# A gated encoder layer: y transposed on all partitions at once, and the first strip begun on half of the tokens

## The chip, the cores and the metric

The kernel runs on one core of one Trainium2 chip. The metric is the device time of one execution in microseconds; the median of three runs before the change is 2567.74 us (2566.76 to 2569.13). TensorE (PE) multiplies matrices and accumulates in PSUM banks, VectorE (DVE) and ScalarE (ACT) work element by element, GpSimd (POOL) here issues transfers and computes a few powers, and SyncE (SP) issues the other transfers.

## The reference

With DEPTH = 1 only one layer is computed, a gated MLP with spatial mixing. x has 1024 tokens of 2048 channels, the inner width E is 4096, the chunks are 128 tokens and there are 8 groups of 512 channels.

```python
h = rmsnorm(x, a_norm)
z = h @ w_in                                  # (1024, 3 * 4096)
u, v, gate = split(z, 3)
u = gelu(u)
v = rmsnorm(gelu(v), v_gain)
vc = v.reshape(b, 8, 128, 8, 512)
sv = einsum('gpq,bnqgc->bnpgc', w_s, vc) + b_s
y = u * sv.reshape(b, 1024, 4096)
x = x + (y * silu(gate)) @ w_out
out = rmsnorm(x, final_norm)
```

## The kernel before

**Products.** Both large matrix products are done as Strassen's seven products of half blocks. A block is named by two digits: of the left operand, the first digit is the half of the tokens (512 of 1024) and the second the half of the inner dimension; of a weight, the first is the half of the inner dimension and the second one of two column blocks of 512. `A_OF` and `B_OF` (lines 20 and 21) give the blocks that each product adds or subtracts; `IN_ORDER` and `OUT_ORDER` the order of the products. Every operand is split into a high part that TensorE takes exactly and a low part that is the remainder (`split`, lines 84 to 87: ACT writes the high part, VectorE subtracts), and each product is three matmuls (`mm3`, lines 89 to 93: high by high, high by low, low by high).

**Steps.** The work is a list of steps (line 108). The input product has 12 strips of two column blocks: four strips of v, then eight strips that pair a group of u with the same group of gate. Each strip has seven products of JI = 4 steps; a step is 2 x 128 of the inner dimension, 24 matmuls of 128x512. The output product has seven products by two column pairs by JO = 8 steps. At each step i, `advance` first issues the loads for step i+3 (`prefetch`) and forms the operands of step i+2 (`feed`); then come the matmuls (`products`), and then `work`, which takes entries from two lists of postponed work, `soon` (taken first, all of it) and `later` (until the costs written beside the entries use up an allowance of 2.3 us, less in part of the output product).

**Banks.** PSUM is used as two sets of four banks. Products 1, 2 and 5 of a strip start on fresh banks; 4 and 7 go on accumulating on product 2's, 3 and 6 on product 5's, after `end_of` has read what it needs of the product before. In the order 1, 2, 5, 4, 3, 7, 6 the two sets alternate (lines 401 to 440).

**Start.** x comes transposed, as 16 tiles of 256 channels by 512 tokens, both halves of the tokens in turn (line 235 and following). Each tile is squared by ACT, its two parts added by VectorE and summed over the channels by a matmul with ones into `ss_x`. From the sums of both halves the reciprocal root mean square is made (`d_x`, a reduction, a power on POOL), spread over the partitions as `r_b` by a matmul with a diagonal matrix for each half, and applied to a block of x when it is first wanted (`h_block`, line 161). `feed_first` forms the first step's operands half by half so that TensorE can begin early. In the first strip each product forms its left operands and POOL writes them to DRAM (`a_dram`); the later strips read them back. Weight blocks are loaded for each product anew in the first strip; from the second on a block that two products of a strip use stays in its buffer.

**Buffers.** Tiles of 4 KB per partition come from four groups of buffers: 25 "big" (x, raw weights, read-back operands, output accumulators), 6 "hl" (split weights), 3 "sum" and 16 "ax".

**Mixing.** v is written to DRAM by strip. For each group, `spatial_step` reads it back, splits it, multiplies it by the mixing matrix, whose rows carry v's norm, and multiplies by u * silu(gate). The output product wants y with channels on partitions, so `finish_y` (line 337) transposes: for each of the 4 chunks of a half of the tokens it takes 4 parts of 32 tokens, and each part is 4 instructions on 32 partitions by 4 blocks of 32 channels. One instruction transposes 32x32 blocks within 32 partitions. The result of two chunks, 128 channel partitions by 4 by 256 tokens, is one transfer to `y_dram`. `load_y` reads it back for the output product; if the last group isn't complete by then, the postponed work is done first.

**Output.** The result is accumulated on top of x, loaded by POOL (`init_acc`, line 453). Rows are squared and summed as they are finished; `scale_rows` and `finish_rows` (line 491) multiply by the final norm and SP stores 128 rows by 512 columns at a time, 32 stores, 16 for each half of the tokens; those of the second half come after the last matmuls.

**Order.** Within an engine, instructions run in one fixed order, made when the program is built. It follows the order of the code, except that an instruction that is not expected to be ready can be passed by a later one.

Of the kernel before, what the change touches and what calls it, by code (L numbers as in the profile page):

```python
# [14 lines left out]
P = 128  # L15
# [15 lines left out]
def gmlp_kernel(ctx, tc, x, xT, g_in, w_in, gain, wsT, bsT, w_out, fnorm, out):  # L31
# [88 lines left out]
    def load_w(step, block):  # L120
        kind, s, p, j = step
        mat, cols, n = (w_in, strips, JI) if kind == "in" else (w_out, outs, JO)
        cached = kind == "in" and s > 0
        key = (kind, s, 0 if cached else p, block, j)
        if key not in wraw:
            k = ((block // 10 - 1) * n + j) * 2 * P
            col = cols[s][block % 10 - 1]
            wraw[key] = slot("big", "w_raw")
            nc.sync.dma_start(
                out=wraw[key], in_=mat[k:k + 2 * P, col:col + C].rearrange("(u p) c -> p u c", p=P))  # L130
        return wraw[key]

    def load_y(step, block):
        _, _, p, j = step
        key = (p, block, j)
        if key not in yraw:
            g, b = divmod(((block % 10 - 1) * JO + j) * 2, CB)
            if g == G - 1 and pairs_of_y[0] < 4 * G:
# [35 lines left out]
    def feed_first():  # L174

        step = steps[0]
        (a1, _, a2), (b1, _, b2) = A_OF[step[2]], B_OF[step[2]]
        aparts[0] = [slot("ax", f"a_{l}", F32R) for l in ("hi", "lo")]
        wparts[0] = [slot("hl", f"w_{l}", F32R) for l in ("hi", "lo")]
        w1, w2 = load_w(step, b1), load_w(step, b2)  # L180
        ws, hs = slot("sum", "w_sum"), slot("sum", "a_sum")
        nc.vector.tensor_tensor(out=ws, in0=w1, in1=w2, op=ALU.add)
        split(ws, *wparts[0])
        for u in range(2):
            t1, t2 = h_block(step, a1, (u,)), h_block(step, a2, (u,))
            nc.vector.tensor_tensor(out=hs[:, u], in0=t1[:, u], in1=t2[:, u], op=ALU.add)
# [47 lines left out]
    ss_x, r_ps = bank_set(1, "ss_x")  # L234
    order_x = [(jj, h) for j in range(JI) for jj in (j, JI + j) for h in range(2)]
    for n, (jj, h) in enumerate(order_x):
        t = hx[jj, h] = slot("big", "x_t")
        nc.sync.dma_start(
            out=t, in_=xT[jj * 2 * P:(jj + 1) * 2 * P, h * HT:(h + 1) * HT].rearrange("(u p) c -> p u c", p=P))
        sq = slot("ax", "sq_x")  # L240
        nc.scalar.activation(out=sq, in_=t, func=AF.Square)
        nc.vector.tensor_tensor(out=sq[:, 0], in0=sq[:, 0], in1=sq[:, 1], op=ALU.add)
        nc.tensor.matmul(out=ss_x[:, h], lhsT=ones[:, 0, :P], rhs=sq[:, 0], start=n < 2, stop=n >= len(order_x) - 2)
# [3 lines left out]
    by_chunk = "p a (b c) -> p (a b) c"
    d_x = slot("ax", "d_x")
    dv = d_x.rearrange(by_chunk, c=P)
    eyes = eye.rearrange("p (a c) -> p a c", a=1).broadcast_to([P, NCH, P])  # L250
    nc.vector.tensor_tensor(out=dv, in0=ss_x.rearrange(by_chunk, c=P), in1=eyes, op=ALU.mult)
    nc.vector.tensor_reduce(out=ss_t, in_=dv, axis=mybir.AxisListType.X, op=ALU.add)
    inv_rms(ss_t, D, rx)

    r_b = slot("sum", "r_b")
    for h in range(2):
        for n in range(HCH):
            nc.vector.tensor_scalar(
                out=d_x[:, h, n * P:(n + 1) * P], in0=eye, scalar1=rx[:, h * HCH + n:h * HCH + n + 1], scalar2=None,
                op0=ALU.mult)  # L260
        nc.tensor.matmul(out=r_ps[:, h], lhsT=ones[:, 0, :P], rhs=d_x[:, h], start=True, stop=True)
        nc.scalar.activation(out=r_b[:, h], in_=r_ps[:, h], func=AF.Copy)

# [43 lines left out]
    def apply_spatial(g, half, n_set, prod):  # L307
# [10 lines left out]
        for m in range(HCH):  # L318
            for part in range(P // Q):
                later.append((1.2, lambda m=m, part=part: finish_y(g, half, m, part, prod[m // 2])))  # L320

# [14 lines left out]

    def finish_y(g, half, m, i, y):

        t, c = divmod(m, 2)
        if c == 0 and i == 0:  # L340
            yts[0] = slot("ax", "y_t").rearrange("p a (b c) -> p (a b) c", c=2 * P)
        yt = yts[0]
        yv = y[:, c].rearrange("t (b q c) -> t b q c", b=CB, q=P // Q)
        for q in range(P // Q):
            nc.vector.transpose(  # L345
                out=yt[q * Q:(q + 1) * Q, :, c * P + i * Q:c * P + (i + 1) * Q],
                in_=yv[i * Q:(i + 1) * Q, :, q, :])
        if c == 1 and i == P // Q - 1:
            nc.gpsimd.dma_start(out=y_dram[g][half][:, :, 2 * t * P:2 * (t + 1) * P], in_=yt)  # L349
            pairs_of_y[0] += 1  # L350

    pairs_of_y = [0]

# [16 lines left out]
    for i in range(1, AHEAD):  # L370
        feed(i)


    i = 0
    before = None
    for s in range(len(strips)):
        is_v = s < NV
        g = s - NV
        a, b = s % 2, (s + 1) % 2
        sets, cs, gains = {}, {}, None  # L380
# [19 lines left out]

        def end_of(p, banks, cs=cs, act=act):

            for t in range(2):
                if p == 1:
                    if t == 0:
                        cs[22] = [slot("ax", f"u{t}") for t in range(2)]
                    soon.append((0, lambda t=t: nc.scalar.activation(out=cs[22][t], in_=banks[t], func=AF.Copy)))
                elif p in (2, 5):
                    soon.append((1.2, lambda t=t: nc.vector.tensor_tensor(
                        out=cs[22][t], in0=cs[22][t], in1=banks[t], op=ALU.subtract)))  # L410
# [42 lines left out]
    def init_acc(s, block):  # L453
# [4 lines left out]
        for t in range(2):  # L458
            r0 = ((block // 10 - 1) * HCH + 2 * t) * P
            nc.gpsimd.dma_start(  # L460
                out=acc[s, block][t], in_=x[r0:r0 + 2 * P, col:col + C].rearrange("(u p) c -> p u c", p=P))

# [28 lines left out]
    def finish_rows(h, m):  # L491

        ro = ros.pop((h, m))
        r0 = (h * HCH + m) * P
        for s in range(2):
            for n in range(2):
# [8 lines left out]
                col = outs[s][n]  # L505
                nc.sync.dma_start(out=out[r0:r0 + P, col:col + C], in_=d)

# [93 lines left out]
```

## Time and profile before

| | |
|---|---|
| median of three runs | 2567.74 us |
| profiled execution, its own time | 2568.74 us |
| span from first to last instruction | 2567.0 us |
| mean granted TensorE clock | 0.994 |
| TensorE busy | 2520.2 us, 98% |
| VectorE busy | 1798.8 us, 70% |
| ScalarE busy | 856.3 us, 33% |
| transposes of y on VectorE | 1024, 309.7 us |
| data moved | 701.92 MB, mean 273 GB/s |

The busy times are shares of the whole span. Matmuls overlap, so a busy TensorE can still issue more slowly than it could; the count of matmuls in a stretch says more than its busy time. The idle time of an engine that isn't the bottleneck costs nothing.

### The profile page before, as it was taken

What the parts mean: (1) busy time and instruction counts of PE and PEld (TensorE: products, weight loads), DVE (VectorE), ACT (ScalarE), POOL (GpSimd) and SP (SyncE); (2) the same over time, 40 slices, a digit from 0 to 9 for tenths busy, and PEclk for the clock granted to TensorE, in tenths of its full rate; (3) what the DMA queues carried; (4) which work ended last, traced back from release to release, by engine and by line L of the source; (5) the groups of instructions that cost most, each with busy time, mean ns of one, the idle gap of its engine ahead of it and who ended that gap; (6) DMA issues with size and microseconds to landing.
All of it is one profiled execution on the core that took longest, in us unless ns stands there. A gap on an engine that the chain in (4) does not pass through costs nothing. (4 is left out here: it accounts for less than half of the span.)

```text
span 2567.0 us, 29706 instructions
## 1 busy us (share of the span) xinstructions
PE 2520.2 (98%) x10980; PEld 2062.7 (80%) x10980; DVE 1798.8 (70%) x2466; ACT 856.3 (33%) x1008; POOL 166.6 (6%) x289
## 2 busy tenths in 40 slices
PE   6999999999999999999999999999999999999998
PEld 3887888888888888888888888888888788888886
DVE  6984454645447859688695885958869854586795
ACT  4452232323324242242422324233243232233342
POOL 1220000000000000000000000000010210010010
PEclk8999999999999999999999999999999999999999
DMA  8998785968867685776857768586696875778885
GB/s 308 344 414 335 255 333 197 383 207 307 299 236 280 239 334 195 284 274 239 332 196 291 263 234 332 205 294 250 234 351 212 298 262 161 230 267 283 294 293 192
DMA packets 250048, 701.92 MB, mean 273 GB/s; under 512 B 21664, under 2 KB 21680, under 8 KB 249904
## 3 DMA queue, kind: packets, MB, share of 16 engines
q1 hardware_dynamic: 210816, 557.91, 60.7%
q0 software_dynamic: 39088, 142.11, 15.0%
q8 instruction: 87, 1.43, 0.2%
q14 instruction: 57, 0.47, 0.1%
HBM read 628.63 MB, written 71.30 MB: 273 GB/s over the span
## 5 line engine op out<-in xcount | busy, mean ns | idle before, releaser
L92 PE MATMUL m<-w_lo,a_hi 128*128 128x512 f32 x2688 | 1049.8, 391 | 11.3 <-DVE w_lo L87 11.3
L91 PE MATMUL m<-w_hi,a_hi 128*128 128x512 f32 x2688 | 1047.7, 390 | 3.7 <-ACT a_hi L86 3.5
L93 PE MATMUL m<-w_hi,a_lo 128*128 128x512 f32 x2688 | 1047.9, 390 | 0.0
L87 DVE TENSOR_TENSOR w_lo<-w_sum,w_hi 128x1024 fp32r<-128x1024 f32 x320 | 391.4, 1223 | 397.6 <-ACT w_hi L86 397.0
L86 ACT ACTIVATE w_hi<-w_sum 128x1024 fp32r<-128x1024 f32 x320 | 339.0, 1060 | 949.0 <-PE m L92 672.4
L92 PEld LDWEIGHTS m<-w_lo,a_hi 128*128 128x128 f32 x2688 | 505.8, 188 | 122.8 <-DVE w_lo L87 18.2
L91 PEld LDWEIGHTS m<-w_hi,a_hi 128*128 128x128 f32 x2688 | 505.6, 188 | 111.7 <-ACT a_hi L86 5.0
L93 PEld LDWEIGHTS m<-w_hi,a_lo 128*128 128x128 f32 x2688 | 505.7, 188 | 105.1 <-DVE a_lo L87 0.6
L101 DVE TENSOR_TENSOR w_sum<-w_raw 128x1024 f32<-128x1024 f32 x319 | 388.9, 1223 | 116.3 <-DMA w_raw<-in_w_in 102.8
L92 PE MATMUL o<-w_lo,a_hi 128*128 128x512 f32 x896 | 350.1, 391 | 4.8 <-DVE w_lo L87 4.8
L91 PE MATMUL o<-w_hi,a_hi 128*128 128x512 f32 x896 | 349.3, 390 | 0.8 <-DVE o L548 0.8
L93 PE MATMUL o<-w_hi,a_lo 128*128 128x512 f32 x896 | 349.3, 390 | 0.0
L345 DVE STREAM_TRANSPOSE y_t<-c 32x128 f32<-32x128 f32 x1024 | 309.7, 302 | 15.1
L86 ACT ACTIVATE w_hi<-w_raw 128x1024 fp32r<-128x1024 f32 x128 | 135.7, 1061 | 449.4 <-PE m L92 347.1
L87 DVE TENSOR_TENSOR w_lo<-w_raw,w_hi 128x1024 fp32r<-128x1024 f32 x128 | 155.7, 1217 | 126.4 <-ACT w_hi L86 125.6
L92 PEld LDWEIGHTS o<-w_lo,a_hi 128*128 128x128 f32 x896 | 168.5, 188 | 42.4 <-DVE w_lo L87 7.7
L91 PEld LDWEIGHTS o<-w_hi,a_hi 128*128 128x128 f32 x896 | 168.6, 188 | 36.8 <-DVE o L548 1.5
L93 PEld LDWEIGHTS o<-w_hi,a_lo 128*128 128x128 f32 x896 | 168.6, 188 | 34.8
L86 ACT ACTIVATE a_hi<-a_sum 128x1024 fp32r<-128x1024 f32 (+1 forms) x61 | 63.6, 1043 | 147.2 <-DVE a_sum L101 145.0
L141 POOL DMA_DIRECT2D y_raw<-y x96 | 51.1, 534 | 468.1 <-DVE w_sum L101 252.0
L87 DVE TENSOR_TENSOR a_lo<-a_sum,a_hi 128x1024 fp32r<-128x1024 f32 (+1 forms) x61 | 73.4, 1205 | 10.2 <-ACT a_hi L86 10.1
L349 POOL DMA_DIRECT2D y<-y_t x32 | 23.1, 723 | 727.0 <-DVE y_t L345 727.0
(90 smaller groups left out, 1112.5 us busy)
## 6 DMA issues: line engine op xcount, KB each, us to landing
w_raw<-in_w_in SPq DMA_DIRECT2D x224, 512.0 KB, 6.7
w_raw<-in_w_out SPq DMA_DIRECT2D x192, 512.0 KB, 6.2
y_raw<-y POOLq DMA_DIRECT2D x96, 512.0 KB, 6.2
a_hi<-a_0h SPq DMA_DIRECT2D x77, 512.0 KB, 4.8
a_lo<-a_0l SPq DMA_DIRECT2D x77, 512.0 KB, 5.3
a_hi<-a_1h SPq DMA_DIRECT2D x77, 512.0 KB, 6.2
a_lo<-a_1l SPq DMA_DIRECT2D x77, 512.0 KB, 5.1
a_hi<-a_2h SPq DMA_DIRECT2D x77, 512.0 KB, 6.0
```

Source lines behind the costliest of these rows:

```text
L86: nc.scalar.activation(out=hi, in_=raw, func=AF.Copy)
L87: nc.vector.tensor_tensor(out=lo, in0=raw, in1=hi.bitcast(F32), op=ALU.subtract)
L91: nc.tensor.matmul(out=acc, lhsT=ah, rhs=bh, start=start, stop=False, skip_group_check=on)
L92: nc.tensor.matmul(out=acc, lhsT=ah, rhs=bl, start=False, stop=False, skip_group_check=on)
L93: nc.tensor.matmul(out=acc, lhsT=al, rhs=bh, start=False, stop=stop, skip_group_check=on)
L101: nc.vector.tensor_tensor(out=s, in0=a, in1=b, op=ALU.add if of[1] > 0 else ALU.subtract)
L141: nc.gpsimd.dma_start(out=yraw[key], in_=y_dram[g][block // 10 - 1][:, b:b + 2, :])
L345: nc.vector.transpose(out=yt[q * Q:(q + 1) * Q, :, c * P + i * Q:c * P + (i + 1) * Q], in_=yv[i * Q:(i + 1) * Q, :, q, :])
L349: nc.gpsimd.dma_start(out=y_dram[g][half][:, :, 2 * t * P:2 * (t + 1) * P], in_=yt)
```

## The change

It has three parts, each with what follows from it.

1. **The transposes of y.** `finish_y` transposes, for each chunk of 128 tokens, all 128 partitions at once by 32x32 blocks, 256 channels in one instruction, two instructions a chunk. The 32 partitions of one quarter then hold channels, for 32 of the chunk's tokens. The four chunks of a half are collected in two tiles, and eight transfers, one for each quarter of the partitions of each tile, put them in their places in `y_dram`, which now is channels by tokens. Within a half the tokens come in the order quarter, chunk, token of 32. So `init_acc` reads x, and `finish_rows` writes the output, in rows of that order: four groups of 32 rows that are 128 rows apart. The reading of y and of `w_out` takes neighbouring channels 2p and 2p+1 on partition p.
2. **The start.** x is loaded, squared and summed for the first half of the tokens, then the first steps' weights are loaded, and the second half's loads and sums come behind the operands of the first two steps. The first strip takes its products in the order 5, 3, 1, 2, 4, 6, 7, of which 5 and 3 need only the first half of the tokens.
3. **What goes with the new order.** The set of banks that each strip starts on; the signs with which `end_of` collects the products of the first strip; and weight block 22, wanted by four products of the first strip (5, 3, 1 and 7), stays in its buffers.

```diff
+FIRST_ORDER = (5, 3, 1, 2, 4, 6, 7)
-    steps = [("in", s, p, j) for s in range(len(strips)) for p in IN_ORDER for j in range(JI)]
+    steps = [("in", s, p, j) for s in range(len(strips)) for p in (IN_ORDER if s else FIRST_ORDER) for j in range(JI)]
-    y_dram = [[dram.tile([P, CB, HT], F32, tag=f"y{g}_{h}", name=f"y{g}_{h}") for h in range(2)] for g in range(G)]
+    y_dram = [[dram.tile([C, HT], F32, tag=f"y{g}_{h}", name=f"y{g}_{h}") for h in range(2)] for g in range(G)]
...
-        cached = kind == "in" and s > 0
+        cached = kind == "in" and (s > 0 or block == 22)
...
+            order = "(u p) c -> p u c" if kind == "in" else "(p u) c -> p u c"
+            nc.sync.dma_start(out=wraw[key], in_=mat[k:k + 2 * P, col:col + C].rearrange(order, p=P))
...
-            nc.gpsimd.dma_start(out=yraw[key], in_=y_dram[g][block // 10 - 1][:, b:b + 2, :])
+            nc.gpsimd.dma_start(
+                out=yraw[key], in_=y_dram[g][block // 10 - 1][b * P:(b + 2) * P].rearrange("(p u) t -> p u t", p=P))
...
+    def load_x(h):
+        for n, jj in enumerate(order_x):
+            t = hx[jj, h] = slot("big", "x_t")
+            nc.sync.dma_start(
+                out=t, in_=xT[jj * 2 * P:(jj + 1) * 2 * P, h * HT:(h + 1) * HT].rearrange("(u p) c -> p u c", p=P))
+            sq = slot("ax", "sq_x")
+            nc.scalar.activation(out=sq, in_=t, func=AF.Square)
+            nc.vector.tensor_tensor(out=sq[:, 0], in0=sq[:, 0], in1=sq[:, 1], op=ALU.add)
+            nc.tensor.matmul(out=ss_x[:, h], lhsT=ones[:, 0, :P], rhs=sq[:, 0], start=n == 0, stop=n == len(order_x) - 1)
+
+    def scale_x(h):
...
+    load_x(0)
     for i in range(LOADS):
         prefetch(i)
+    scale_x(0)
...
-    def finish_y(g, half, m, i, y):
-        t, c = divmod(m, 2)
-        if c == 0 and i == 0:
-            yts[0] = slot("ax", "y_t").rearrange("p a (b c) -> p (a b) c", c=2 * P)
-        yt = yts[0]
-        yv = y[:, c].rearrange("t (b q c) -> t b q c", b=CB, q=P // Q)
-        for q in range(P // Q):
-            nc.vector.transpose(
-                out=yt[q * Q:(q + 1) * Q, :, c * P + i * Q:c * P + (i + 1) * Q],
-                in_=yv[i * Q:(i + 1) * Q, :, q, :])
-        if c == 1 and i == P // Q - 1:
-            nc.gpsimd.dma_start(out=y_dram[g][half][:, :, 2 * t * P:2 * (t + 1) * P], in_=yt)
-            pairs_of_y[0] += 1
+    def finish_y(g, half, m, y):
+        if m == 0:
+            yts[0] = [slot("ax", f"y_t{n}").rearrange("p a (b c) -> p (a b) c", c=P) for n in range(2)]
+        yv = y.rearrange("t (n b c) -> t n b c", n=2, c=Q)
+        for n in range(2):
+            nc.vector.transpose(out=yts[0][n][:, :, m * Q:(m + 1) * Q], in_=yv[:, n])
+        if m == HCH - 1:
+            yd = y_dram[g][half].rearrange("(n b c) t -> n c b t", n=2, c=Q)
+            for n in range(2):
+                for q in range(P // Q):
+                    nc.gpsimd.dma_start(out=yd[n, :, :, q * P:(q + 1) * P], in_=yts[0][n][q * Q:(q + 1) * Q])
+            halves_of_y[0] += 1
...
     feed_first()
     for i in range(1, AHEAD):
         feed(i)
+    load_x(1)
+    scale_x(1)
...
-        a, b = s % 2, (s + 1) % 2
+        a = (s - 1) % 2 if s else 0
+        b = 1 - a
...
+                if s == 0 and p in (5, 1):
+                    if t == 0 and p == 5:
+                        cs["u"] = [slot("ax", f"u{t}") for t in range(2)]
+                    if p == 5:
+                        soon.append((0, lambda t=t: nc.scalar.activation(
+                            out=cs["u"][t], in_=banks[t], func=AF.Copy, scale=-1.0)))
+                    else:
+                        soon.append((1.2, lambda t=t: nc.vector.tensor_tensor(
+                            out=cs["u"][t], in0=cs["u"][t], in1=banks[t], op=ALU.add)))
...
-        for p in IN_ORDER:
+        for p in IN_ORDER if s else FIRST_ORDER:
             fresh = p in (1, 2, 5)
+            if s == 0:
+                work(0)
             if fresh:
-                sets[p] = bank_set(b if p == 2 else a, f"m{p}")
+                sets[p] = bank_set(b if p == 2 or (s == 0 and p == 1) else a, f"m{p}")
...
+    rows = "(h m q t) d -> h q m t d"
+    xv, ov = [r.rearrange(rows, h=2, m=HCH, t=Q) for r in (x, out)]
...
-            r0 = ((block // 10 - 1) * HCH + 2 * t) * P
-            nc.gpsimd.dma_start(
-                out=acc[s, block][t], in_=x[r0:r0 + 2 * P, col:col + C].rearrange("(u p) c -> p u c", p=P))
+            for u in range(2):
+                nc.gpsimd.dma_start(
+                    out=acc[s, block][t][:, u], in_=xv[block // 10 - 1, 2 * t + u, :, :, col:col + C])
...
-                nc.sync.dma_start(out=out[r0:r0 + P, col:col + C], in_=d)
+                nc.sync.dma_start(out=ov[h, m, :, :, col:col + C], in_=d)
```

`scale_x(h)` does for one half of the tokens what was done for both: `ss_x` by the identity, the reduction, mean and power for 4 chunks, the diagonals, the matmul with ones and the copy to `r_b`.

More of the change, by code (lines that the diff above doesn't have):

```diff
@@ L137, in load_y @@
             g, b = divmod(((block % 10 - 1) * JO + j) * 2, CB)
-            if g == G - 1 and pairs_of_y[0] < 4 * G:
+            if g == G - 1 and halves_of_y[0] < 2 * G:
                 work_all()
             yraw[key] = slot("big", "y_raw")
-            nc.gpsimd.dma_start(out=yraw[key], in_=y_dram[g][block // 10 - 1][:, b:b + 2, :])
+            nc.gpsimd.dma_start(
+                out=yraw[key], in_=y_dram[g][block // 10 - 1][b * P:(b + 2) * P].rearrange("(p u) t -> p u t", p=P))
         return yraw[key]
@@ L176, in feed_first @@
         step = steps[0]
-        (a1, _, a2), (b1, _, b2) = A_OF[step[2]], B_OF[step[2]]
+        (a1, _, a2), (b1,) = A_OF[step[2]], B_OF[step[2]]
         aparts[0] = [slot("ax", f"a_{l}", F32R) for l in ("hi", "lo")]
         wparts[0] = [slot("hl", f"w_{l}", F32R) for l in ("hi", "lo")]
[L180 to L183, printed above, removed]
+        split(load_w(step, b1), *wparts[0])
+        hs = slot("sum", "a_sum")
         for u in range(2):
@@ L234, in gmlp_kernel @@
     ss_x, r_ps = bank_set(1, "ss_x")
[L235 to L243, printed above, removed]
+    r_b = slot("sum", "r_b")
@@ new lines, in gmlp_kernel @@
+    d_x = slot("ax", "d_x")
+    dv = d_x.rearrange("p a (b c) -> p a b c", c=P)
+    eyes = eye.rearrange("p (a c) -> p a c", a=1).broadcast_to([P, HCH, P])
+    order_x = [jj for j in range(JI) for jj in (j, JI + j)]
+    def load_x(h):
[7 more added lines that the diff above has]
+            nc.tensor.matmul(out=ss_x[:, h], lhsT=ones[:, 0, :P], rhs=sq[:, 0], start=n == 0, stop=n == len(order_x) - 1)
@@ new lines, in scale_x @@
+    def scale_x(h):
+        cs = slice(h * HCH, (h + 1) * HCH)
+        nc.vector.tensor_tensor(
+            out=dv[:, h], in0=ss_x[:, h].rearrange("p (b c) -> p b c", c=P), in1=eyes, op=ALU.mult)
+        nc.vector.tensor_reduce(out=ss_t[:, cs], in_=dv[:, h], axis=mybir.AxisListType.X, op=ALU.add)
+        nc.vector.tensor_scalar(
+            out=m_all[:, cs], in0=ss_t[:, cs], scalar1=1.0 / D, scalar2=EPS, op0=ALU.mult, op1=ALU.add)
+        nc.gpsimd.tensor_tensor(out=rx[:, cs], in0=m_all[:, cs], in1=mhalf[:, cs], op=ALU.pow)
+        for n in range(HCH):
+            nc.vector.tensor_scalar(
+                out=dv[:, h, n], in0=eye, scalar1=rx[:, h * HCH + n:h * HCH + n + 1], scalar2=None, op0=ALU.mult)
+        nc.tensor.matmul(out=r_ps[:, h], lhsT=ones[:, 0, :P], rhs=d_x[:, h], start=True, stop=True)
+        nc.scalar.activation(out=r_b[:, h], in_=r_ps[:, h], func=AF.Copy)
@@ L244, in gmlp_kernel @@
+    load_x(0)
     for i in range(LOADS):
         prefetch(i)
[L247 to L262, printed above, removed]
+    scale_x(0)
@@ L318, in apply_spatial @@
         for m in range(HCH):
-            for part in range(P // Q):
-                later.append((1.2, lambda m=m, part=part: finish_y(g, half, m, part, prod[m // 2])))
+            later.append((0.8, lambda m=m: finish_y(g, half, m, prod[m // 2][:, m % 2])))
     def spatial_step(k, g, cs, n_set):
@@ L335, in gmlp_kernel @@
     yts = {}
[L337 to L352 removed]
+    def finish_y(g, half, m, y):
[10 more added lines that the diff above has]
+            halves_of_y[0] += 1
+    halves_of_y = [0]
     def products(i, banks, fresh, ms=range(4)):
@@ L417, in end_of @@
                     block = 11 if p == 7 else 22
-                    if t == 0 and p == 7:
-                        cs[11] = [slot("ax", f"c11_{t}") for t in range(2)]
+                    if t == 0:
+                        us = cs["u"]
+                        new = p == (6 if s == 0 else 7)
+                        cs[block] = [slot("ax", f"c{block}_{t}") for t in range(2)] if new else us
                     def last(t=t, block=block):
-                        nc.vector.tensor_tensor(out=cs[block][t], in0=cs[22][t], in1=banks[t], op=ALU.add)
+                        nc.vector.tensor_tensor(out=cs[block][t], in0=us[t], in1=banks[t], op=ALU.add)
                         act(block, t, cs[block][t])
                     soon.append((1.2, last))
-        for p in IN_ORDER:
+        for p in IN_ORDER if s else FIRST_ORDER:
             fresh = p in (1, 2, 5)
+            if s == 0:
+                work(0)
             if fresh:
-                sets[p] = bank_set(b if p == 2 else a, f"m{p}")
+                sets[p] = bank_set(b if p == 2 or (s == 0 and p == 1) else a, f"m{p}")
             chain = sets[{4: 2, 7: 2, 3: 5, 6: 5}.get(p, p)]
```

13 lines of the change are left out of this document (5 added, 8 removed).

## The prediction

> **What bounds the kernel now.** I read the page's busy times first, then TensorE's busy time by stretches, then its waits, then the start and the end in order of time.
>
> ```profile
> PE 2520.2 (98%) x10980; PEld 2062.7 (80%) x10980; DVE 1798.8 (70%) x2466; ACT 856.3 (33%) x1008; POOL 166.6 (6%) x289
> ```
>
> TensorE is the bound, and it computes the same matmuls afterwards. So only its lost time can move: before the first product, in holes, and after the last one. The stretches (PE, weight load, DVE, ACT, POOL busy with counts, granted clock, DMA share, GB/s) say where that is:
>
> ```profile
> 40.00:60.00 20.00, 15.50 (x51) 10.79 (x50) 19.79 (x25) 6.02 (x7) 3.46 (x7) 0.76 0.64 225
> 200.00:210.00 10.00, 6.02 (x23) 4.59 (x22) 3.01 (x3) 2.12 (x2) 0.00 (x0) 0.83 1.04 406
> 210.00:220.00 10.00, 10.00 (x39) 8.08 (x38) 8.29 (x9) 5.53 (x11) 0.53 (x1) 0.83 1.03 409
> 400.00:600.00 200.00, 200.00 (x884) 165.62 (x883) 99.88 (x91) 58.70 (x79) 4.80 (x9) 1.00 0.71 258
> 850.00:900.00 50.00, 49.34 (x218) 40.27 (x217) 42.71 (x84) 9.55 (x9) 3.05 (x5) 1.00 0.72 251
> 900.00:950.00 50.00, 50.00 (x222) 41.42 (x221) 26.42 (x25) 19.06 (x21) 0.54 (x1) 1.00 0.88 330
> 1800.00:1850.00 50.00, 49.36 (x217) 40.29 (x216) 44.63 (x91) 10.77 (x11) 3.26 (x5) 1.00 0.72 242
> 1950.00:2000.00 50.00, 48.25 (x212) 39.18 (x211) 48.62 (x88) 10.24 (x11) 5.91 (x9) 1.00 0.71 245
> 2000.00:2050.00 50.00, 46.90 (x197) 37.52 (x197) 43.67 (x71) 13.16 (x13) 9.80 (x17) 0.97 0.86 301
> 2555.00:2560.00 5.00, 1.65 (x8) 1.03 (x6) 2.99 (x9) 2.72 (x7) 0.91 (x2) 1.00 0.94 350
> ```
>
> A full stretch issues 884 matmuls in 200 us, 0.226 us each, or 222 in 50 us. Against that the turn from first to second strip (200 to 220) loses 92-62 = 30 matmuls, 6.8 us. Seven stretches like 850 to 900 and 1800 to 1850, about one a strip, lose 4 or 5 each, some 7.5 us together. The turn to the output product, 1950 to 2050, loses 35, 7.9 us. In all of these but the first turn VectorE is the cause:
>
> ```profile
> PE m L92 <- DVE w_lo L87: 11.3, 11, 4.0
> PE o L92 <- DVE w_lo L87: 4.8, 5, 2.0
> ```
>
> Its 4.0 is the first turn, where w_lo is late because its load is. The start, in order of time:
>
> ```profile
> 16.19 1.06 ACT L241 ACTIVATE sq_x<-x_t 128x1024 f32<-128x1024 f32 x1 [0.31 <-DMA x_t<-in_xT]
> 27.10 1.06 ACT L241 ACTIVATE sq_x<-x_t 128x1024 f32<-128x1024 f32 x1 [0.37 <-DMA x_t<-in_xT]
> 28.18 0.69 DVE L242 TENSOR_TENSOR sq_x<-sq_x 128x512 f32<-128x512 f32 x1 [0.74 <-ACT sq_x L241]
> 30.17 1.23 DVE L251 TENSOR_TENSOR d_x<-ss_x,ones 128x1024 f32<-128x1024 f32 x1 [1.29 <-PE ss_x L243]
> 31.43 1.22 DVE L252 TENSOR_REDUCE ss_t<-d_x 128x8 f32<-128x1024 f32 x1
> 33.01 1.68 POOL L82 TENSOR_TENSOR rx<-m_all,mhalf 128x8 f32<-128x8 f32 x1 [29.12 <-DVE m_all L81]
> 37.76 0.60 ACT L262 ACTIVATE r_b<-ss_x 128x512 f32<-128x512 f32 x1 [9.61 <-PE ss_x L261]
> 38.40 1.41 DVE L169 SCALAR_TENSOR_TENSOR x_t<-x_t,g_sb,r_b 128x512 f32<-128x512 f32 x2 [0.88 <-ACT r_b L262]
> 42.49 1.28 DVE L186 TENSOR_TENSOR a_sum<-x_t 128x512 f32<-128x512 f32 x2
> 43.95 0.79 PE L91 MATMUL m<-w_hi,a_hi 128*128 128x512 f32 x1 [3.46 <-ACT a_hi L86]
> 45.56 2.73 DVE L169 SCALAR_TENSOR_TENSOR x_t<-x_t,g_sb,r_b 128x512 f32<-128x512 f32 x4
> 66.66 1.23 DVE L87 TENSOR_TENSOR w_lo<-w_sum,w_hi 128x1024 fp32r<-128x1024 f32 x1
> ```
>
> Sixteen x tiles are squared, the last from 27.10; the chain to r_b follows; the first product is at 43.95. Then VectorE is the bound until the fourth step's operands are split, at 66.66+1.23 = 67.9.
>
> **The start, part by part.** Products 5 and 3 need only the first half of the tokens, so the path ends with the eighth tile (16.19) and not the sixteenth (27.10): 10.9 us. d_x and its reduction work on half the width: 0.69 for 1.23 (the L242 row), and about 0.65 for 1.22: 1.1. The power on 4 columns, between 0.84 (the same operation on one column) and 1.68, I take at 1.2: 0.5. Before, a_sum comes 42.49-38.40 = 4.1 after r_b, since block 22 waits for the second half's r_b; both blocks are now of the first half, and 1.4 is left: 2.7. Sum 15.2: r_b at about 25.9, first product at 28.7.
>
> ```profile
> L82 POOL TENSOR_TENSOR ro<-m_inv,mhalf 128x1 f32<-128x1 f32 x8 | 6.7, 844 | 68.0 <-DVE m_inv L81 63.4 <-DVE ss L487 4.5
> L409 DVE TENSOR_TENSOR u<-u,m 128x1024 f32<-128x1024 f32 x48 | 58.0, 1218 | 12.5 <-PE m L93 11.6
> L345 DVE STREAM_TRANSPOSE y_t<-c 32x128 f32<-32x128 f32 x1024 | 309.7, 302 | 15.1
> L349 POOL DMA_DIRECT2D y<-y_t x32 | 23.1, 723 | 727.0 <-DVE y_t L345 727.0
> ```
>
> VectorE gives some of it back. Four steps of product 5 need four norms (2.73), a_sum and a_lo (1.2 each) a step, 20.6, and the last w_lo, 1.2; the earlier w_lo fit before 25.9, their three loads standing right behind the eight tiles. The second half's eight additions (0.69 each, 5.5) and its d_x, reduction and diagonals (2.5) go to the same engine. 25.9+29.8 = 55.7 against 67.9: 12.2 of the 15.2 are left at the fourth step. The second half's eight sums on TensorE, about 1.1 us each, fall where it waits for VectorE anyway; without that cover they cost up to 9.
>
> The new order makes three products begin on banks that were finished a moment ago (3 on 5's, 2 on 1's, 4 on 2's). The reader of the bank takes 1.2 us (L409's row; the copy by ACT I count alike), a pair of banks is finished six matmuls, 1.4 us, before the product ends, and it may stand behind one other VectorE instruction: between 0 and 2.4 each, I take 0.8, +2.4 in all. Queued behind it are the splits for the next step, which have two steps' lead.
>
> The turn at 200 to 220 is a transfer's:
>
> ```profile
> 205.61 1.22 DVE L101 TENSOR_TENSOR w_sum<-w_raw 128x1024 f32<-128x1024 f32 x1 [4.96 <-DMA w_raw<-in_w_in]
> w_raw<-in_w_in SPq DMA_DIRECT2D x224, 512.0 KB, 6.7
> ```
>
> Keeping block 22 takes away 12 of these loads (3 for each of the 4 values of j), 6.3 MB, 15 us at 406 GB/s; but TensorE is there 10 us earlier. Between 0 and 6.8, I take 2 won. The kept tiles occupy four of the nine buffers that x leaves; the other five hold at least two steps. Sum of the start: -12.2+2.4-2 = **-11.8** (-5 to -17).
>
> **The transposes.** 1024 of 302 ns become 128 on all partitions with 256 elements each instead of 128. Bounds: 302 ns each (39 us), or the eight old blocks one after the other (310 us, no gain). From 512 elements (0.69, the L242 row) to 1024 (1.218, L409) an operation grows by 0.53 us, 1.03 ns an element; if partitions go side by side as in every other row here, that is 302+132 = 434 ns, 56 us in all, which I take. 254 us leave VectorE, 32 a strip. Of the 7.5 us in the strips I count 6.5 won, of the 7.9 at the output turn 5.5, since part of that is a late read of y:
>
> ```profile
> 2021.67 1.23 DVE L101 TENSOR_TENSOR a_sum<-y_raw 128x1024 f32<-128x1024 f32 x1 [4.37 <-DMA y_raw<-y]
> L460 POOL DMA_DIRECT2D o<-in_x x16 | 11.5, 738 | 39.0 <-DVE w_lo L87 27.7 <-DVE a_sum L101 6.7 <-DMA w_raw<-in_w_out 4.6
> ```
>
> **-12** (0 to -15). For it POOL issues 128 stores of y instead of 32, each of 256 pieces; L460 has 256 pieces and takes 738 ns, so 94 us in place of 23, on an engine that is 6% busy. Behind a store that waits stand the reads of v and y; those of the last group are wanted over ten steps later. Without that cover the price is a wait like the 4.37.
>
> **The end.** The joined quarters leave tokens in another order, so x is read and the output written as 4 groups of 32 rows, 128 rows apart. Before, both sides of a store count 128 rows outermost.
>
> ```profile
> 2487.88 0.97 SPq L506 DMA_DIRECT2D out<-o  x2
> 2492.96 0.95 SPq L506 DMA_DIRECT2D out<-o  x2
> 2494.00 14.96 SPq L129 DMA_DIRECT2D w_raw<-in_w_out  x14
> 2551.82 0.41 SPq L506 DMA_DIRECT2D out<-o_fn  x1
> 2562.12 0.40 SPq L506 DMA_DIRECT2D out<-o_fn  x1
> out<-o SPq DMA_DIRECT2D x28, 256.0 KB, 3.8
> 2501.08 1.23 DVE L101 TENSOR_TENSOR w_sum<-w_raw 128x1024 f32<-128x1024 f32 x1 [0.50 <-DMA w_raw<-in_w_out]
> ```
>
> The last 16 stores, 16 x 256 KB = 4.19 MB, are issued from about 2551 to 2562.5 and saturate the engines even now: 350 GB/s at a share of 0.94 (2555 to 2560) is 372 when full, 23.3 an engine, 11.3 us for all. No row shows a transfer with 4 outermost. Bounds: it is spread as before, 0; or it is dealt out by its outermost count, to four engines: 93 GB/s, 45 us, ending at 2551+45 = 2596 instead of 2562.1+0.4+2.7 = 2565.2 (the o_fn stores land in 2.7): +30.8. I take the upper end: 4 is the only count that both sides can be divided by at their outermost dimension, and nothing follows that could hide it. The nearest row by bytes, the old store, speaks for 0; hence a large chance for the first rival.
>
> The Trainium skill, "DMA: Bandwidth & Descriptors", section "Why a DMA increments its semaphore by 16 and not by 1", says that a transfer uses the largest number of engines up to 16 which divides the slowest dimension of both sides. By it the stores run on four engines and the sum is the one I take; read by the old store's row it would be the first rival's. No run here shows it yet.
>
> The first four stores also stand ahead of the last weight loads on the SP queue (2488 to 2494). On four engines they take 11 us there, 8 more than now, and the load for the step at hand is already waited for (0.50 at 2501.08). Between 0 and 7, I take +3. Reading x in 32 pieces on POOL costs 0 under three steps of prefetch, up to 3 without. The end: **+34** (+28 to +40, or 0).
>
> **Sum.** The profiled execution took 2568.74 us for a span of 2567.0, 1.0 above the median of 2567.74. 2568.7-11.8-12+34 = 2578.9; less 1.0, 2577.9, so **2578 us**.
>
> **The rivals.** (1) The stores still use 16 engines, the change is faster: 2578-34 = 2544. For it: same bytes, queue and 2 KB rows as the stores that land in 3.8 us. Against it: the outermost count. (2) The early start is eaten: the second half's squares, additions and sums stand ahead of the first products in the fixed queues of ACT, VectorE and TensorE, so the first product waits for the last x tile after all. It then starts about 8 us later, at 36 to 37, and with the bank waits at 2.4 each some 2 are left of the 11.8: 2578+10 = 2588. For it: VectorE is full from 40 on. Against it: in the rows its order already goes past instructions that are not ready.
>
> **Chances.** Forecast 0.62 (2564 to 2587 its own range), rival 1 0.26 (2535 to 2553), rival 2 0.12. Less than 0.2% (5 us) can't be told from no change. Faster: 0.25 of rival 1 and 0.04 of the forecast; same: 0.18 of the forecast, 0.01 each of the rivals; slower: 0.40 and 0.11. The range 2541 to 2590 leaves out about a third of rival 1 and the upper ends.
>
> **What will show it.** First product near 29 us and the fourth step's operands near 56 (rival 2: 37 and 65). L345's successor x128 at about 434 ns. Stretches like 850 to 900 with 222 matmuls. Stores of the output landing in over 10 us at a DMA share near 0.25 after the last matmul, for some 45 us; rival 1: near 0.9 and gone within 15. The prediction is wrong if the share stays high there, or if TensorE starts before 32 us and is not ahead by 200.

## The result and the profile after

The changed kernel takes 2591.56 us (median of four runs, 2590.37 to 2600.08) against 2567.61 before (four runs): a ratio of 1.0100, 95% interval 1.0088 to 1.0112, so it is slower by 24 us. The forecast was 2578, and the range ended at 2590. The profiled execution is the fastest of the four, 2590.37 us with a span of 2588.3, which is 21.3 longer than the span before; the account below explains these 21.3 us. In the experiments, one run of f1 (11472 us) and one of the kernel before beside it (3164 us) took far longer than the others and are left out of the ratios.

The page of the changed kernel gives the busy times (engine, us, share, instructions). Below it stand one of its groups and two of TensorE's waits. L355 is the successor of L345.

```profile
PE 2513.8 (97%) x10980; PEld 2066.2 (80%) x10980; DVE 1534.5 (59%) x1573; ACT 855.0 (33%) x1008; POOL 228.0 (9%) x402
...
L355 DVE STREAM_TRANSPOSE y_t<-c 128x256 f32<-128x256 f32 x128 | 43.6, 406 | 0.0
...
PE o L94 <- DVE w_lo L89: 8.5, 3, 3.9
PE m L93 <- DVE u L433: 6.1, 1, 6.1
```

VectorE is 264 us less busy. The 128 transposes take 406 ns each; as those that follow one another overlap, they keep VectorE busy for 43.6 us and not for 128 x 0.406 = 52. One wait of TensorE, 6.1 us on the subtraction `u`, is new. The waits for `w_lo` in the output product were 4.8 us before and are 8.5 now: some 5.8 at the turn to the output product, the rest between 2400 and 2500. Where the time went is read by counting matmuls in stretches. First the same stretches of the kernel before (PE, weight load, DVE, ACT, POOL busy with counts, granted clock, DMA share, GB/s):

```profile
0.00:100.00 100.00, 77.67 (x251) 48.16 (x252) 78.80 (x98) 43.89 (x44) 15.74 (x32) 0.91 0.89 319
100.00:160.00 60.00, 60.00 (x267) 49.67 (x266) 54.25 (x50) 29.96 (x35) 14.81 (x28) 1.00 0.99 384
160.00:220.00 60.00, 56.02 (x237) 45.80 (x236) 42.12 (x42) 27.55 (x45) 8.51 (x16) 0.94 1.03 412
220.00:1950.00 1730.00, 1725.48 (x7598) 1424.70 (x7597) 1183.88 (x1782) 561.74 (x650) 61.34 (x100) 1.00 0.74 270
2400.00:2500.00 100.00, 100.00 (x443) 82.81 (x442) 83.47 (x93) 35.87 (x49) 14.13 (x22) 1.00 0.83 288
```

Then those of the changed kernel, with the hole's ten microseconds, the output turn and the end:

```profile
0.00:100.00 100.00, 81.03 (x288) 55.24 (x289) 82.85 (x106) 52.17 (x58) 20.18 (x38) 0.93 0.86 312
100.00:160.00 60.00, 53.47 (x226) 43.45 (x225) 47.37 (x44) 19.77 (x20) 10.61 (x20) 0.94 0.99 366
130.00:140.00 10.00, 3.95 (x12) 2.90 (x11) 6.25 (x6) 1.06 (x1) 0.53 (x1) 0.73 1.04 416
160.00:220.00 60.00, 60.00 (x267) 49.67 (x266) 46.57 (x46) 30.42 (x47) 10.08 (x19) 1.00 1.03 408
220.00:1950.00 1730.00, 1730.00 (x7634) 1432.51 (x7633) 960.01 (x999) 563.47 (x651) 116.17 (x202) 1.00 0.74 270
1950.00:2000.00 50.00, 50.00 (x223) 41.39 (x222) 31.84 (x27) 12.51 (x12) 12.24 (x21) 1.00 1.03 281
2000.00:2050.00 50.00, 44.25 (x180) 35.62 (x179) 27.93 (x24) 13.10 (x13) 9.37 (x16) 0.93 1.04 277
2400.00:2500.00 100.00, 97.15 (x422) 79.71 (x421) 79.76 (x93) 36.85 (x50) 13.08 (x22) 0.98 0.81 282
2560.00:2580.00 20.00, 0.00 (x0) 0.00 (x0) 0.00 (x0) 0.00 (x0) 0.00 (x0) 0.50 0.26 102
```

At 0.226 us a matmul the two tables make a ledger:

| stretch | matmuls after against before | us |
|---|---|---|
| 0 to 100 | 288 against 251 | -8.4 |
| 100 to 160 | 226 against 267 | +9.3 |
| 160 to 220 | 267 against 237 | -6.8 |
| 220 to 1950 | 7634 against 7598 | -8.1 |
| 1950 to 2050 | 403 against 409 (212+197) | +1.4 |
| 2400 to 2500 | 422 against 443 | +4.7 |
| together, at the last matmul | | -7.9 |

The stretches left out, 2050 to 2400 and 2500 to 2540, differ by one matmul each. The last matmul bears the sum out: it starts at 2548.28, and before at 2556.26. The span grew by 21.3, so what follows the last matmul grew by 21.3+7.9 = 29.2 us. There the mean share of the 16 DMA engines is 0.26 at 102 GB/s with nothing else running, about a quarter.

**The hole at 131 us**, in order of time:

```profile
123.92 12.84 SPq L133 DMA_DIRECT2D w_raw<-in_w_in  x6
134.57 1.23 DVE L103 TENSOR_TENSOR w_sum<-w_raw 128x1024 f32<-128x1024 f32 x1 [3.75 <-DMA w_raw<-in_w_in]
135.71 2.34 DVE L433 TENSOR_TENSOR u<-u,m 128x1024 f32<-128x1024 f32 x2
137.07 0.76 PE L93 MATMUL m<-w_hi,a_hi 128*128 128x512 f32 x1 [6.05 <-DVE u L433]
```

Product 4 goes on in product 2's banks, so it needs L433 to have read them. L433 stands behind a weight sum on VectorE, and that sum waits for its load. The operands of product 4 are ready; the reader of its banks isn't. The lower granted clock (0.73 in 130 to 140) adds to it: the stretch has 41 matmuls fewer, 9.3 us, for a wait of 6.05 us.

**The output turn.** y is read late. These are VectorE's waits for it over the whole run (us, times, longest), before and after, and the row of the reads of x after:

```profile
DVE a_sum L101 <- DMA y_raw<-y: 18.7, 9, 4.4
```

```profile
DVE a_sum L103 <- DMA y_raw<-y: 33.1, 14, 6.4
...
o<-in_x POOLq DMA_DIRECT2D x32, 256.0 KB, 13.5
```

A read of x (`o<-in_x`) of 256 KB now lands 13.5 us after its issue (median), where 512 KB took 8.6 before.

### The profile page after: what moved, and what is told of

It is laid out like the page before. It is cut to its first block, busy times and chain, and to the rows that moved or that the text cites. A ratio compares the mean times of both kernels' runs of the same rounds, so it can differ in the third digit from the quotient of the medians.

```text
span 2588.3 us, 28945 instructions
## 1 busy us (share of the span) xinstructions
PE 2513.8 (97%) x10980; PEld 2066.2 (80%) x10980; DVE 1534.5 (59%) x1573; ACT 855.0 (33%) x1008; POOL 228.0 (9%) x402
## 4 chain that ended last, share of the span: by engine, by line
PE 88%; DMA 6%; DVE 3%; issue 1%; POOL 0%; ACT 0%; SPq 0%; POOLq 0%; ACTq 0%; DVEq 0%
PE m L93 23%; PE m L94 23%; PE m L95 23%; PE o L94 6%; PE o L95 6%; PE o L93 6%; DMA y_raw<-y 3%; DMA w_raw<-in_w_in 1%; DMA o<-in_x 1%; DMA w_raw<-in_w_out 1%; DVE w_lo L89 1%; PE sv L94 0%; PE sv L93 0%; PE sv L95 0%; DMA x_t<-in_xT 0%
## 5 line engine op out<-in xcount | busy, mean ns | idle before, releaser
L360 POOL DMA_DIRECT2D y<-y_t x128 | 74.0, 586 | 406.7 <-DVE y_t L355 392.6
L298 POOL DMA_DIRECT2D v_raw<-v x32 | 17.4, 544 | 660.5 <-DVE ws_hl L313 642.8
```

Of the source, the lines that this page charges most:

```text
L298: nc.gpsimd.dma_start(out=spatial["v", c], in_=v_dram[g][h][:, 2 * t:2 * t + 2])
L360: nc.gpsimd.dma_start(out=yd[n, :, :, q * P:(q + 1) * P], in_=yts[0][n][q * Q:(q + 1) * Q])
```

## Experiments

### The stores alone, in two steps

In e1 to e4, e6, g1 and g2 rows of x or of the output stand beside other tokens than the products that they meet; the amount of work and of data is the same, but for e6's repeated loads.

e1 stores to 128 neighbouring rows:

```diff
-                nc.sync.dma_start(out=ov[h, m, :, :, col:col + C], in_=d)
+                r0 = (h * HCH + m) * P
+                nc.sync.dma_start(out=out[r0:r0 + P, col:col + C], in_=d)
```

> The changed kernel, but each store writes 128 neighbouring rows as before, so its destination counts 128 rows outermost (the rows of the output then stand in another order). Number of stores, bytes and 2 KB rows stay. Theory (a store is dealt out to as many engines as its outermost count of 4 allows): the last 16 stores take some 12 us after 2544 instead of 44, at a DMA share near 0.9, and the weight loads at 2490 no longer wait behind stores: 2591.6 - 29 - 4.5 = 2558. Rival (the end is long because stores are issued late or because of the order of the products): the end stays, within 3 us of 2591.6.

e4 stores to 8 groups of 16 rows:

```diff
-                nc.sync.dma_start(out=ov[h, m, :, :, col:col + C], in_=d)
+                o8 = out[h * HT:(h + 1) * HT].rearrange("(g m t) d -> m g t d", g=8, m=HCH)
+                nc.sync.dma_start(out=o8[m, :, :, col:col + C], in_=d)
```

> The changed kernel, but each store writes 8 groups of 16 rows instead of 4 of 32 (the rows of the output then stand in another order). Theory (engines by the outermost count): eight engines, 186 GB/s, 22.5 us for the last 16 stores from 2544, so the end comes 21 us sooner, at 2544 + 22.5 + 2 and some: 2570, and a DMA share near 0.5 at the end. Rival (rows that lie apart are slow to write, in smaller groups more so): 2591 or more.

e1 measured 2554.24 (2547.53 to 2557.14), ratio to before 0.9946 (0.9927 to 0.9964); e4 measured 2565.9 (2555.3 to 2569.52), 0.9986 (0.9975 to 0.9997). Both lie some 4 us below what was expected. The stretch 2540 to 2545 of e1, and the stretch 2545 to 2550 of e4, in both of which the last stores are being written:

```profile
2540.00:2545.00 5.00, 0.00 (x0) 0.00 (x0) 3.36 (x8) 3.39 (x6) 0.54 (x1) 0.83 0.88 330
```

```profile
2545.00:2550.00 5.00, 3.01 (x12) 2.18 (x12) 3.56 (x10) 3.36 (x7) 0.78 (x2) 1.00 0.52 189
```

Four groups give a share of 0.26, eight 0.52 and 128 rows 0.88. The packet records of the traces show what the share stands for: in the changed kernel 4 or 5 packets are under way at any time between 2560 and 2580, in e4 8 to 10 between 2550 and 2560, and a packet of 2 KB takes 84 ns in both. So the number of groups decides how many engines carry a store, as the prediction took it. The Trainium skill, "DMA: Bandwidth & Descriptors", section "Why a DMA increments its semaphore by 16 and not by 1", states that count as the largest divisor of both slowest dimensions up to 16; the three shares agree with 4, 8 and 16.

### The reads of x

e2 reads x from 128 neighbouring rows, e3 does that and e1's edit:

```diff
-                    out=acc[s, block][t][:, u], in_=xv[block // 10 - 1, 2 * t + u, :, :, col:col + C])
+                r0 = ((block // 10 - 1) * HCH + 2 * t + u) * P
+                nc.gpsimd.dma_start(out=acc[s, block][t][:, u], in_=x[r0:r0 + P, col:col + C])
```

> The changed kernel, but each of the 32 reads of x takes 128 neighbouring rows (x is then added to other tokens than it belongs to). Theory (the reads of x with 4 outermost slow down all transfers at the turn to the output product, 1960 to 2050, where packets take almost twice their time): packets there keep 84 and 159 ns, the 9.5 us that TensorE loses between 2000 and 2200 fall to under 3: 2591.6 - 7 = 2584.6. Rival (y is read late because of its new layout and its 128 stores of 512-byte pieces): the loss stays, 2591.6 within 2.

> Both of the two edits before together (x and output rows in another order). Theory: the two savings add, 2591.6 - 33.5 - 7 = 2551, which is 16 under the kernel before. Rival: one of them has another cause, and 2558 or 2585 remains.

e2 measured 2580.79 (2578.11 to 2582.91), ratio 1.0050 (1.0034 to 1.0066); e3 2547.06 (2546.22 to 2548.31), 0.9920 (0.9906 to 0.9935). These two, too, lie some 4 us below what was expected. The same edit is worth 2591.56-2580.79 = 10.8 us with the slow stores and 2554.24-2547.06 = 7.2 with the quick ones; the second is the rougher of the two, as e1's own four runs lie up to 9.6 us apart. The output turn of e2 is full:

```profile
2000.00:2050.00 50.00, 50.00 (x222) 41.42 (x221) 26.54 (x23) 14.52 (x14) 8.49 (x16) 1.00 0.76 283
```

Counted over the 100 us from 1950 in one piece, e2 and e3 have 443 matmuls, and the profiled executions with POOL's reads in 4 groups have 401 (after), 413 (e1) and 383 (e4), so what the reads cost differs from one to the next. The stores are worth e2-e3 = 33.7 us; 29.2+4.7 = 33.9 stand in the ledger for the tail and for the weight loads behind the first four stores.

What do the reads do to the others? The transfers of 1955 to 2055 us, first after, then e3. A line gives packets, MB and the time that they took as a share of 16 engines; q1 carries the transfers issued by SP, q0 those issued by POOL.

```profile
DMA packets 13856, 27.32 MB, mean 273 GB/s; under 512 B 4066, under 2 KB 4066, under 8 KB 13852
...
q1 hardware_dynamic: 6672, 12.85, 51.4%
q0 software_dynamic: 7180, 14.42, 49.2%
```

```profile
DMA packets 10130, 25.76 MB, mean 258 GB/s; under 512 B 894, under 2 KB 894, under 8 KB 10126
...
q1 hardware_dynamic: 6293, 12.12, 36.9%
q0 software_dynamic: 3833, 13.59, 36.1%
```

SP's packets, which carry the same weights in both, take 0.514 x 1600/6672 = 123 ns each in the one and 0.369 x 1600/6293 = 94 ns in the other. 3172 more packets of under 512 B come along; by the packet records 3072 of them hold 8 bytes and stand in POOL's queue, and e2, e3 and the kernel before have none of these. The shares of the two queues add up to all 16 engines' time (51.4+49.2%) for about the data that takes 73% of it in e3. So reads in 4 groups don't only run slowly themselves, they slow the y and weight transfers beside them. Two more runs asked why.

g1 is e1 with x read as 8 groups of 16 rows, g2 is e1 with the reads in 4 groups issued by SP:

```diff
+                hb = block // 10 - 1
+                x8 = x[hb * HT:(hb + 1) * HT].rearrange("(g m t) d -> m g t d", g=8, m=HCH)
                 nc.gpsimd.dma_start(
-                    out=acc[s, block][t][:, u], in_=xv[block // 10 - 1, 2 * t + u, :, :, col:col + C])
+                    out=acc[s, block][t][:, u], in_=x8[2 * t + u, :, :, col:col + C])
```

> The changed kernel with its output stored to neighbouring rows (e1, 2554.2), and x read as 8 groups of 16 rows instead of 4 groups of 32 (the rows of x then stand beside other tokens' products, the work is the same). If the number of groups is the number of DMA engines that carry a read, and their crowding is what slows every packet, twice the engines take away half or more of the 7.2 us that e3 is ahead of e1: 2547 to 2551, packets at 1960 to 1980 us between 159 and 275 ns. If the scattered rows as such are the cause, 2554 and packets of 275 ns as before.

```diff
-                nc.gpsimd.dma_start(
+                nc.sync.dma_start(
                     out=acc[s, block][t][:, u], in_=xv[block // 10 - 1, 2 * t + u, :, :, col:col + C])
```

> The changed kernel with its output stored to neighbouring rows (e1, 2554.2), with the reads of x in 4 groups issued by SP instead of POOL. If it takes POOL's queue and the 8-byte packets that come with each of its reads to slow the others, packets of 2 KB at 1960 to 1980 us go back to some 84 ns and the time to about 2547 (e3), unless the weight loads behind them on SP come late. If four engines carrying the reads are enough, the packets stay at 150 ns or more and the time at 2554.

g1 measured 2544.11 (2543.6 to 2544.91), 0.9906 (0.9891 to 0.9921), which is 3 us below the bottom of what either theory gave; it is no slower than e3. g2 measured 2558.87 (2556.31 to 2560.43), 0.9962 (0.9947 to 0.9977), no faster than e1 (the intervals overlap). The same 100 us, g1 first, then g2:

```profile
DMA packets 11392, 26.66 MB, mean 267 GB/s; under 512 B 1872, under 2 KB 1872, under 8 KB 11388
...
q1 hardware_dynamic: 6433, 12.39, 43.2%
```

```profile
DMA packets 9979, 23.81 MB, mean 238 GB/s; under 512 B 682, under 2 KB 682, under 8 KB 9975
...
q1 hardware_dynamic: 7383, 14.32, 46.8%
...
PE o L94 <- DVE w_lo L89: 9.8, 2, 6.4
```

With 8 groups a packet of q1 takes 0.432 x 1600/6433 = 107 ns, between e3 and after, and small packets are 978 more than in e3 instead of 3172: TensorE no longer loses a matmul to it (222 and 223 in the two stretches of 50 us from 1950). The scattered rows as such are therefore not the cause; the effect falls with the number of groups. With SP as issuer the small packets are no more than in e3 and a packet of q1 takes 0.468 x 1600/7383 = 101 ns. But now the weight loads queue behind the reads, TensorE waits 9.8 us for w_lo, and the gain is lost another way. So the crowding in the changed kernel comes with POOL's reads in few groups. In g2 fewer transfers also ran side by side, because the weight loads stood in line behind the reads. That isn't the whole reason: of the packets that began in these 100 us while 18 or more were under way, one of 2 KB takes 100 ns in g2 (median), 139 in e1 and 87 in e3. Whether POOL's small packets cause the rest stays open, since they came and went with POOL's reads in few groups.

### The start alone, and the transposes

e5 is the kernel before with the new start and nothing else of the change. f1 has the whole change, but puts the tokens back in order where y's operands are summed and split, so that x and the output go by 128 neighbouring rows (x as it was before, e1's stores):

```diff
+                order = lambda v: v.rearrange("p (q m t) -> p m q t", m=HCH, t=Q)
+                plain = lambda v: v.rearrange("p (m q t) -> p m q t", m=HCH, t=Q)
...
+                        nc.vector.tensor_tensor(
+                            out=plain(raw[:, u]), in0=order(ys[0][:, u]), in1=order(ys[1][:, u]),
+                            op=ALU.add if A_OF[p][1] > 0 else ALU.subtract)
...
+                    nc.scalar.activation(out=hi, in_=order(raw[:, u]), func=AF.Copy)
+                    nc.vector.tensor_tensor(
+                        out=lo, in0=order(raw[:, u]), in1=hi.bitcast(F32), op=ALU.subtract)
```

> The kernel before with the new start alone: first half of x first, order 5, 3, 1, 2, 4, 6, 7 in the first strip, block 22 kept; transposes, y, x and output as before. The prediction's term: -11.8, so 2556. What the changed kernel's count of matmuls up to 220 us says: 24 more than before, -5.4, so 2562. If the start gained nothing: 2567.7.

> The changed kernel with the tokens put back in order inside the core: where y's operands are summed or split for the output product, VectorE and ScalarE read each half as quarter, chunk, 32 tokens and write it as chunk, quarter, 32 tokens. x and the output are read and written as 128 neighbouring rows, as before the change, and the result is the reference's. Theory (the loss lies only in transfers with 4 outermost): 2547 as with both row orders undone, within 3, although VectorE does two instructions of half the width for each of 56 steps. Rival (reading 32 elements at a stretch makes these instructions slow, or they delay the splits): 2555 or more.

e5 measured 2562.37 (2560.5 to 2563.88), 0.9979 (0.9970 to 0.9989): the start is worth 5 us. f1 measured 2547.72, 0.9918 (0.9900 to 0.9936). f1 lies 2562.37-2547.72 = 14.7 us below e5, and that is what the transposes are worth when no transfer goes in groups; e5 and f1 have the hole at 131 us both.

### The hole: order or buffers

Two theories of the hole at 131 us: (A) the product that continues product 2's banks comes too early, so put another between; (C) the kept tiles of block 22 hold buffers, so the load is issued late. Against both stands (B): the transfer engines can't deliver the first strip's weights in time. f2 is f1 with another order; e6 is e3 without the keeping, f3 is f1 without it, f4 has both.

```diff
-FIRST_ORDER = (5, 3, 1, 2, 4, 6, 7)
+FIRST_ORDER = (5, 3, 1, 2, 6, 4, 7)
```

> The kernel with the tokens put back in order, and the first strip's products in the order 5, 3, 1, 2, 6, 4, 7, so that product 6 stands between 2 and 4. Theory A (the hole at 131 to 137 is a wait in VectorE's fixed order: the subtraction that frees product 2's banks stands behind a weight sum that waits for its load): the hole of 6 us and its 2 us of lower clock go, 2540. Theory B (the transfers can't deliver the first strip's weights in time, whatever stands in the queue): the hole comes back at another step as a wait for w_lo or a bank, 2547 within 2.

```diff
-        cached = kind == "in" and (s > 0 or block == 22)
+        cached = kind == "in" and s > 0
```

> The changed kernel with 128 neighbouring rows for x and output (rows in another order), and block 22 not kept in the first strip: four buffers more for loads, 12 loads (6.3 MB) more. Theory C (loads are issued too late because the kept tiles hold four of nine buffers): the wait for w_raw near 131 to 135 goes, 2540. Theory B (the transfer engines are full): the wait grows or comes back at the turn to the second strip, 2550 to 2560.

> The kernel that puts the tokens back in order in VectorE (f1, 2547.7), and block 22 is loaded again for every product instead of being kept. If the kept tiles are what makes the loads at 124 to 134 us late, the same 6.3 us go as in e6 against e3: 2541. If keeping block 22 is a saving (6.3 MB fewer at the start) and e6 was a chance of its two executions: 2547 or more.

> f1 with both repairs of the start: the order 5, 3, 1, 2, 6, 4, 7 of f2 and block 22 not kept. If both repairs remove one and the same hole (131 to 137 us), they do not add: 2538 to 2542, where the lower end is f2's 15 missing matmuls of 160 to 220 us (3.4 us) coming back. If they were two independent gains of 6 us each: 2535.5.

| | median | ratio to before | difference, us |
|---|---|---|---|
| f1 | 2547.72 | 0.9918 (0.9900 to 0.9936) | |
| f2, order | 2541.82 | 0.9899 (0.9883 to 0.9915) | -5.9 to f1 |
| e6, not kept | 2540.77 | 0.9894 (0.9873 to 0.9915) | -6.3 to e3 |
| f3, not kept | 2539.87 | 0.9889 (0.9875 to 0.9904) | -7.9 to f1 |
| f4, both | 2539.86 | 0.9890 (0.9873 to 0.9906) | 0 to f3 |

e6 has two runs only; f3 repeats its edit with four. f3 and f4 ran in another round than f1, in which the kernel before took 2568.54 and not 2567.29; by the ratios f3 lies 7.4 us below f1.

The stretch of the hole in f1 and in f2, in which only the order differs:

```profile
100.00:160.00 60.00, 54.78 (x230) 44.60 (x229) 46.75 (x43) 20.76 (x21) 10.60 (x20) 0.94 0.98 367
```

```profile
100.00:160.00 60.00, 59.52 (x263) 48.99 (x262) 50.49 (x47) 21.09 (x21) 10.61 (x20) 1.00 0.98 366
```

f2 then has 14 matmuls fewer between 160 and 220 (252, where f1 has 266); f4 has 262 there. f3 in the stretches of the start:

```profile
0.00:100.00 100.00, 81.11 (x287) 55.32 (x288) 82.77 (x105) 52.17 (x58) 20.18 (x38) 0.93 0.96 363
100.00:160.00 60.00, 59.24 (x260) 48.47 (x260) 52.96 (x51) 27.48 (x33) 12.19 (x23) 1.00 1.00 382
160.00:220.00 60.00, 60.00 (x266) 49.67 (x266) 42.40 (x42) 26.41 (x38) 8.49 (x17) 1.00 1.03 414
```

Which readers of a buffer SP's queue waited for at 100 to 160 us, in f1 and in f3 (us in total, times, longest):

```profile
SPq L133 <- DVE w_lo L89: 19.3, 4, 6.5
SPq L133 <- DVE w_sum L103: 17.0, 7, 4.9
SPq L133 <- DVE a_sum L103: 5.4, 3, 3.6
```

```profile
SPq L133 <- DVE w_lo L89: 18.8, 4, 6.5
SPq L133 <- DVE w_sum L103: 11.1, 6, 4.1
SPq L133 <- DVE a_sum L103: 2.7, 1, 2.7
```

TensorE's wait for the bank is 4.7 us in f1, 0.3 in f3 and none in f2 and f4. Each repair takes the hole away and the two don't add, so it is one hole with two conditions: a late load, and a reader of the banks queued behind it. Theory B fails: loading block 22 again moves 6.3 MB more and is still faster. SP waits 32.6 us for buffers instead of 41.7 in these 60 us. By 220 us f3 has 813 matmuls against 755 before: 58, or 13.1 us. f3 beats both kernels, by 1.1% the one before.

## Why the prediction was wrong

In the prediction's own terms, measured by the ledger:

| term | predicted | measured | |
|---|---|---|---|
| start | -11.8 | -5.9 | e5: -4.9 |
| strips | -6.5 | -8.1 | |
| output turn | -5.5 | +1.4 | e2 lies 10.8 lower, e3 7.2 below e1 |
| weight loads behind the first stores | +3 | +4.7 | |
| stores after the last matmul | +30.8 | +29.2 | |
| sum | +10.0 | +21.3 | span +21.3 |

Of the 11.3 us between the two sums, 6.9 are the output turn's and 5.9 the start's; the other three come to -1.5 together.

**The step that failed first: "Reading x in 32 pieces on POOL costs 0 under three steps of prefetch, up to 3 without."** It asked only whether the reads themselves would come in time. The prediction applied the count of groups to the stores and not to the reads, which have the same four. In the runs the reads take the gain of 5.5 at the output turn away and 1.4 more, since y's reads beside them come late. With this one edit undone (e2) the time is 10.8 us lower, 2580.79, inside the forecast's own range.

**The second: "the other five hold at least two steps", with the bank waits "between 0 and 2.4 each".** The wait for a bank was priced as its reader behind at most one other VectorE instruction. It was a longer queue: the reader behind a weight sum, that behind a load, that behind buffers which the kept tiles held. It came to 6.05 us, and to 41 matmuls, 9.3 us, with the lower clock; +2.4 was put down for all three such waits together. Keeping block 22 was counted as a saving of transfers in the turn at 200 to 220; that turn was indeed won (6.8, where 2 was taken), but f3 wins it too (266 matmuls between 160 and 220), without keeping anything.

The prediction had named a sign for this: it is wrong if TensorE starts before 32 us and is not ahead by 200. TensorE started at 31.34, and by 200 the changed kernel has 689 matmuls and the kernel before 692. The whole lead of the start is made in the 20 us after that, at the turn to the second strip. f3, without the hole, has 723 by 200.

**The early start itself.** The first product began at 31.34, not 28.7:

```profile
19.42 0.68 DVE L258 TENSOR_TENSOR d_x<-ss_x,ones 128x512 f32<-128x512 f32 x1
20.02 1.21 DVE L89 TENSOR_TENSOR w_lo<-w_raw,w_hi 128x1024 fp32r<-128x1024 f32 x1
21.15 0.68 DVE L260 TENSOR_REDUCE ss_t<-d_x 128x4 f32<-128x512 f32 x1
21.75 1.22 DVE L89 TENSOR_TENSOR w_lo<-w_raw,w_hi 128x1024 fp32r<-128x1024 f32 x1
27.32 0.60 ACT L268 ACTIVATE r_b<-ss_x 128x512 f32<-128x512 f32 x1 [6.36 <-PE ss_x L267]
31.34 0.80 PE L93 MATMUL m<-w_hi,a_hi 128*128 128x512 f32 x1 [4.06 <-ACT a_hi L88]
56.03 1.22 DVE L89 TENSOR_TENSOR a_lo<-a_sum,a_hi 128x1024 fp32r<-128x1024 f32 x1
```

"The earlier w_lo fit before 25.9" holds, but two of them stand inside the chain to r_b, which ends at 27.9 and so 2.0 later. The fourth step's operands are ready at 56.03+1.22 = 57.3, forecast 55.7. TensorE is 8.4 us ahead at 100, of the 12.2 put down for the fourth step; 1.6 of the difference is this delay, and no run here separates the rest. Rival 2 (37 and 65) did not come about: the engines did pass the second half's work.

**What held.** The transposes take 406 ns (434 was taken) and 43.6 us in all (56); the strips won 8.1 us, where they were taken to lose 7.5 in all and 6.5 were counted as won. The stores run at a share of 0.26 for the time worked out; rival 1's 0.9 shows where the output goes to neighbouring rows (0.88 in e1). The prediction's argument for four engines had one slip: 4 is the largest count that divides both sides of the store, not the only one. The weight loads were late as said, by 4.7 where 3 was taken:

```profile
2493.79 1.22 DVE L103 TENSOR_TENSOR w_sum<-w_raw 128x1024 f32<-128x1024 f32 x1 [3.73 <-DMA w_raw<-in_w_out]
```

So the sign and the largest term were right. The size missed by two covers that were assumed and not checked against what else shares them: the transfer engines at the output turn, and the buffers at the start.

## What to carry to other kernels

When an access is regrouped, apply the count of the outermost dimension to every transfer that takes the new pattern, loads too, and ask who else is using the engines while they run. Price a wait for a bank by the whole queue that stands ahead of its reader on that engine, down to the load and the buffer that the first of them waits for. A tile kept to save a load is paid for in buffers: here 6.3 MB of repeated loads were cheaper than holding them.

## What was not expected of the hardware

Reads of x in 4 groups, issued by POOL, lengthen SP's packets too, from 94 to 123 ns over 100 us, and bring 3172 packets of under 512 B with them; reads in 8 groups 107 ns and 978, issued by SP 101 ns and fewer than in e3. What the packets of 8 bytes among them are no run here shows. And stores in 4 groups hold SP's queue once earlier ones are still under way: at the end the issue of one takes 2.40 us, where it took 0.40 before. The first four take 0.59 to 0.68 us each (1.35 us for two at 2474.87, 1.18 for two at 2479.95), so it isn't the issue by itself that is long.

```profile
2573.95 2.40 SPq L537 DMA_DIRECT2D out<-o_fn  x1
```
